# A DiT block on one core: the first head's weights split while the modulation columns load, and the upward stage in another unit order

## The chip, the cores and the metric

The kernel runs on one core of a Trainium2 chip. The metric is the device time of one execution in microseconds (us), the median of several runs; one further execution was recorded by the hardware profiler and left a trace.

## The reference

One transformer block of a diffusion model: 2048 rows of x and 256 rows of context, width 1024, 4 HGRN2 heads and 4 retention heads of width 128, a feed-forward width of 2816.

```python
mod = silu(c) @ w_mod + b_mod                    # [1024] @ [1024, 6144]; the same for c_ctx
sh1, sc1, g1, sh2, sc2, g2 = split(mod, 6)
hx = rmsnorm(x, norm1_g) * (1 + sc1) + sh1       # the same for ctx, with its own modulation
p = hx @ w_in                                    # [2048, 1024] @ [1024, 4608], for 8 heads
...                                              # bidirectional chunk scans of HGRN2 and retention,
                                                 # which start from the context's final states
x = x + g1 * (mixed @ w_out)
hx2 = rmsnorm(x, norm2_g) * (1 + sc2) + sh2
gate, up = split(hx2 @ w_up, 2)                  # [2048, 1024] @ [1024, 5632]
gate = conv3_along_rows(gate) + conv_b           # three taps for each column
x = x + g2 * ((silu(gate) * up) @ w_down)        # [2048, 2816] @ [2816, 1024]
return rmsnorm(x, final_g)
```

## The kernel before

**Products.** The large products run in f16 at close to f32 precision: each operand is scaled by a power of two and kept as a pair of f16 numbers (the rounded value and what is left of it), and one product of two blocks is three matmuls (`mm3`, L101 to L103). On top of that a 2x2 block product takes 7 block products instead of 8: rows and contraction, or columns and contraction, are halved, and sums and differences of the halves are formed. So every group of features becomes 7 feature blocks and every pair of weight tiles 7 weight blocks ("w_z", "w_q", "w_vg" for the heads, "w" for the feed-forward), each as an f16 pair. A head's weights come as raw f32 tiles of 128 columns ("raw"), are squared and summed (ssqw) for the power of two (p2s), and then *split*: rounded on ScalarE (`w <- raw, p2s`), the rest formed on VectorE by scalar_tensor_tensor (`w <- raw, p2s, w`, L697), with four subtractions of raw tiles in between.

**Program order.** The kernel is written for a tile framework: tiles live in named slots, waits are put in by dependence, and the framework's scheduler orders the instructions of each engine. Python code sets what comes early or late: generators do a piece of work per step, and `work(n)` lets those in the list `bg` do n steps between the products of a unit.

**Start.** `setup` loads small vectors; `mod_loads` queues on SyncE the first four 512-column blocks of w_mod in the order j4 = 2, 3, 0, 1 (scale, then shift), after j4 = 3 the last group of 512 rows of x (x3, the tiles "hc" and "x"), and raw weight tiles of head 0 (`items0`): z (the two forget gates), q, and v and g together (vg). `heads` calls `mod_first`, which multiplies the columns by silu(c) on TensorE and copies a row of the result from ScalarE (`modrow`, L255), then `norm_rows` (RMS norm of the rows, L398 and L407), the split of z, `lower_bounds` (a softmax, with two table loads of ScalarE), and `modulation`: the vectors A and B of the affine map, the sum of squares and maximum, a power of two s, and A and B times s. `first_blocks` makes the first seven feature blocks of rows 1536 to 2047 ("hx"): transpose the normed rows on TensorE (tp), apply the affine map (ftmp), and form the pairs: the cast on ScalarE (L434), the rest on VectorE (L435). With `early=1` the first chunk is mapped by the unscaled vectors and scaled afterwards. Then q and vg are split, and the heads' projections begin.

**Upward stage.** After the output projection the second norm makes two sets of seven feature blocks ("feat", 1024 rows each; t = 0 and 1; `second_norm_a` and `second_norm_b`, L1481 and L1504). `ffn_up` then walks 22 column tiles in 11 pairs j. For each pair there are four units: ty = 0 (gate) and ty = 1 (up), for both row sets t. A unit (j, ty, t) is 7 block products of 12 matmuls. `up_weights(j, ty)` loads two raw tiles (wur), squares them into two of its own weight tiles, sums them on TensorE (L1596) and splits them, with the four subtractions on GpSimd. Weight tiles have two sets of slots ("z" tags), so the weights of a unit pair can be made while the ones before are used. `gate_evac` applies the convolution taps (L1675 and L1676), `up_evac` multiplies, `act_pairs` forms and stores pairs of the result (st, actd).

The order of the units before is (0,0,0), (0,0,1), (0,1,0), (0,1,1), (1,0,0), ...; the features of set t = 1 are background work of the first unit.

## Time and profile before

| | |
|---|---|
| median of 3 runs | 2621.72 us (2617.08 to 2621.84) |
| profiled execution | 2617.45 us, of which the span is 2615.7 us |
| TensorE (PE) busy | 2509.6 us, 96% of the span |
| VectorE (DVE) busy | 1887.9 us, 72% |
| ScalarE (ACT) busy | 1348.6 us, 52% |
| GpSimd (POOL) busy | 424.9 us, 16% |
| DMA | queue q1 42.4% of 16 engines' time; 152 GB/s over the span |

Busy time is the union of an engine's instructions. The page also has each engine's busy share in 40 slices of the span and the clock that the throttle granted to TensorE ("PEclk"). The span begins with the first recorded instruction; the execution's own time has 1.75 us around it. The first product of the upward stage is at 1368.4 us.

### The profile page before, as it was taken

The page shows a single profiled execution, that of the slowest core. Times are in us where ns is not written, and L with a number is a line of the kernel's source. Part 1 is how long each engine was busy: PE and PEld are TensorE (multiplying, and loading weights), DVE is VectorE, ACT ScalarE, POOL GpSimd, SP SyncE. Part 2 cuts the span into 40 slices and gives each one's busy share as a digit, 9 for nine tenths or more (in the row PEclk, how much of TensorE's full clock was granted, in tenths as well). Part 3 has the DMA queues.
Part 4 walks back from the last instruction along what each step waited for, and adds up shares of the span by engine and source line. Part 5 has one row for each costly group of instructions (what it writes and reads, how often), then busy time and mean ns, then how long its engine had stood idle before and what let it go on. Part 6 is the DMA issues. An engine that isn't in the chain of part 4 may idle for free. (4 is left out here: it accounts for less than half of the span.)

```text
span 2615.7 us, 56265 instructions
## 1 busy us (share of the span) xinstructions
PE 2509.6 (96%) x22763; PEld 1653.6 (63%) x22763; DVE 1887.9 (72%) x4276; ACT 1348.6 (52%) x2877; POOL 424.9 (16%) x409
## 2 busy tenths in 40 slices
PE   5799998999999999999998999999999999999998
PEld 3689887889899999895543444444444444444443
DVE  4888786776878777785658788788888887223756
ACT  5886566564654454553646555556555554211220
POOL 1100000000000000001453433434343432000000
PEclk7999999999999999999999999999999999999999
DMA  8324442442548667794511323233333326544552
GB/s 297 122 86 164 133 143 86 135 148 73 175 163 277 210 225 242 238 343 150 170 72 57 117 89 121 89 113 105 109 105 117 111 99 232 203 175 154 210 208 86
DMA packets 218516, 402.36 MB, mean 154 GB/s; under 512 B 16143, under 2 KB 98291, under 8 KB 213648
## 3 DMA queue, kind: packets, MB, share of 16 engines
q1 hardware_dynamic: 208704, 381.81, 42.4%
q10 hardware_dynamic: 9248, 16.79, 2.0%
q8 instruction: 178, 2.92, 0.5%
q14 instruction: 82, 0.67, 0.1%
q0 software_dynamic: 304, 0.17, 0.0%
HBM read 302.77 MB, written 95.94 MB: 152 GB/s over the span
## 5 line engine op out<-in xcount | busy, mean ns | idle before, releaser
L101 PE MATMUL pa<-feat,w 128*128 128x512 f16 x704 | 265.5, 381 | 9.8 <-ACT ta L597 6.8
L102 PE MATMUL pa<-feat,w 128*128 128x512 f16 x704 | 268.2, 381 | 0.0
L103 PE MATMUL pa<-feat,w 128*128 128x512 f16 x704 | 267.6, 381 | 0.0
L102 PE MATMUL pd<-wd,actl 128*128 128x512 f16 x616 | 233.3, 379 | 0.0
L103 PE MATMUL pd<-wd,actl 128*128 128x512 f16 x616 | 233.3, 379 | 0.0
L101 PE MATMUL pd<-wd,actl 128*128 128x512 f16 x616 | 232.6, 379 | 0.0
L102 PEld LDWEIGHTS <-w 128*128 128x128 f16 x1232 | 120.7, 98 | 153.6 <-issue 15.2
L103 PEld LDWEIGHTS <-w 128*128 128x128 f16 x1232 | 120.8, 98 | 146.4 <-issue 2.1
L101 PEld LDWEIGHTS <-w 128*128 128x128 f16 x1232 | 120.7, 98 | 142.1 <-issue 2.4
L102 PEld LDWEIGHTS <-hx 128*128 128x128 f16 x1824 | 179.3, 98 | 7.3 <-issue 5.1
L101 PEld LDWEIGHTS <-hx 128*128 128x128 f16 x1824 | 179.8, 99 | 2.1
L103 PEld LDWEIGHTS <-hx 128*128 128x128 f16 x1824 | 179.4, 98 | 0.9
L1462 POOL TENSOR_TENSOR ssq<-ssq 128x1 f32<-128x1 f32 x16 | 4.2, 263 | 1066.4 <-ACT junk L1457 1066.4
L1706 DVE SCALAR_TENSOR_TENSOR st<-act,modT,st 128x512 f16<-128x512 f32 x154 | 141.2, 952 | 30.0 <-ACT st L1705 29.3
L1705 ACT ACTIVATE st<-act,modT 128x512 f16<-128x512 f32 x154 | 107.4, 717 | 105.9 <-DVE act L1695 60.4
L101 PE MATMUL pa<-w_vg,hx 128*128 128x128 f16 x800 | 143.0, 220 | 1.0 <-ACT ct L597 0.7
L102 PE MATMUL pa<-w_vg,hx 128*128 128x128 f16 x800 | 142.9, 220 | 0.0
L103 PE MATMUL pa<-w_vg,hx 128*128 128x128 f16 x800 | 142.8, 220 | 0.0
L101 PE MATMUL pc<-feat,w 128*128 128x512 f16 x352 | 133.6, 380 | 2.8 <-ACT tb L597 1.5
L102 PE MATMUL pc<-feat,w 128*128 128x512 f16 x352 | 133.6, 380 | 0.1
L103 PE MATMUL pc<-feat,w 128*128 128x512 f16 x352 | 133.7, 380 | 0.0
L101 PE MATMUL pa<-hx,w_z 128*128 128x256 f16 x464 | 127.1, 274 | 1.6 <-DVE K L639 1.2
(552 smaller groups left out, 7354.1 us busy)
## 6 DMA issues: line engine op xcount, KB each, us to landing
hx<-hxd SPq DMA_DIRECT2D x212, 512.0 KB, 5.0
actd<-st SPq DMA_DIRECT2D x154, 256.0 KB, 2.1
actl<-actd SPq DMA_DIRECT2D x28, 1024.0 KB, 5.2
wur<-in_w_up_dram SPq DMA_DIRECT2D x44, 512.0 KB, 4.1
raw<-in_w_in_dram SPq DMA_DIRECT2D x36, 512.0 KB, 4.8
wm<-in_w_mod_dram SPq DMA_DIRECT2D x64, 256.0 KB, 3.9
hxd<-hx SPq DMA_DIRECT2D x28, 512.0 KB, 4.5
wdb<-in_w_down_dram SPq DMA_DIRECT2D x44, 256.0 KB, 3.9
```

The source lines that it names most:

```text
L101: mm(ps, lhs(0), rhs(0), start=start, stop=False, skip_group_check=True)
L102: mm(ps, lhs(0), rhs(1), start=False, stop=False, skip_group_check=True)
L103: mm(ps, lhs(1), rhs(0), start=False, stop=stop, skip_group_check=True)
L1462: nc.gpsimd.tensor_tensor(ssq[:, 0:1], ssq[:, 0:1], ssq[:, 1:2], ALU.add)
L1705: nc.scalar.activation(p[:, 0], v, AF.Copy, scale=s)
L1706: nc.vector.scalar_tensor_tensor(p[:, 1], v, s, p[:, 0], ALU.mult, ALU.subtract)
```

## The change

1. The host lays out w_in, w_up (tiles of 128 columns) and w_mod (tiles of 512 columns) so that each partition's part of a tile is one piece of memory (4 KB); before, it was pieces of 512 bytes (w_in, w_up) or 2 KB (w_mod).
2. z is loaded first and split before `mod_first(2)`; x3 is loaded after the column j4 = 2; q and vg are loaded after j4 = 3, into other slots, and split before the columns 0 and 1 are worked on; `lower_bounds` and the row norm are written earlier.
3. `first_blocks(plain=True)`: all eight chunks are mapped by the unscaled vectors, the pairs of the blocks 0 and 1 are made after all transposes, and the scale s is applied in the pair itself (an activation with a scale, and scalar_tensor_tensor in the place of tensor_tensor). Six of the eight affine operations are on ScalarE, two on VectorE.
4. In the second norm the feature halves that GpSimd formed are formed by VectorE: in `second_norm_a` all, in `second_norm_b` three of the blocks.
5. The weights W(0,0) go into the slots "vg", which the heads have left; pair 1's gate weights are loaded before the last output product; the units begin (0,0,0), (1,0,0), (0,0,1), (0,1,0), (0,1,1), (1,0,1), (1,1,0), (1,1,1) and go on as before from j = 2.

Lines of the diff, without those around them (of `ffn_up` only the new body; the old one stands above):

```diff
-        wsrc = self.I["w_mod"][0].rearrange("(k p) n -> p k n", p=P)
-        self.wm = []
+        self.items0[0][0]()
+        self.wm = {}
...
+            self.wm[j4] = []
...
-                nc.sync.dma_start(w, wsrc[:, k:k + 2, 512 * j4:512 * j4 + 512])
-                self.wm += [(j4, k + i, w[:, i]) for i in range(2)]
-            if j4 == 3:
+                nc.sync.dma_start(w, self.I["w_mod"][j4, :, k:k + 2])
+                self.wm[j4] += [w[:, i] for i in range(2)]
+            if j4 == 2:
...
-            if j4 in (3, 1):
-                self.items0[0 if j4 == 3 else 4][0]()
-    def mod_first(self):
-        nc = self.nc
-        for j4, k, w in self.wm:
-            if k == 0:
-                ps = self.ps("sc", [P, 512], "mod_ps")
+            if j4 == 3:
+                self.items0[4][0]()
+                self.items0[5][0]()
+    def mod_first(self, j4):
+        nc = self.nc
+        ps = self.ps("sc", [P, 512], "mod_ps")
+        for k, w in enumerate(self.wm[j4]):
...
-            if k == KT - 1:
-                if j4 == 2:
-                    self.small_vectors()
-                self.mod_rows(ps, 2, j4)
+        if j4 == 2:
+            self.small_vectors()
+        self.mod_rows(ps, 2, j4)
...
-            cast = nc.scalar.copy(o[:, :, 0], v)
-            self.tail = nc.vector.tensor_tensor(o[:, :, 1], v, o[:, :, 0], ALU.subtract), cast
+            if plain:
+                cast = nc.scalar.activation(o[:, :, 0], v, AF.Copy, scale=s)
+                self.tail = nc.vector.scalar_tensor_tensor(o[:, :, 1], v, s, o[:, :, 0], ALU.mult, ALU.subtract), cast
+            else:
+                cast = nc.scalar.copy(o[:, :, 0], v)
+                self.tail = nc.vector.tensor_tensor(o[:, :, 1], v, o[:, :, 0], ALU.subtract), cast
...
-        b = []
+        A, B, s = self.plain if plain else self.mod1
+        late, b = [], []
...
-                    A, B, s = self.plain if k < early else self.mod1
-                    A, B = (v[:, which, kk:kk + 1] for v in (A, B))
-                    if r and g in (None, NG - 1):
-                        nc.vector.tensor_scalar(at[r], tp, A, B, ALU.mult, ALU.add)
+                    ka, kb = (v[:, which, kk:kk + 1] for v in (A, B))
+                    if r and (g is None or plain and i):
+                        nc.vector.tensor_scalar(at[r], tp, ka, kb, ALU.mult, ALU.add)
...
-                        nc.scalar.activation(at[r], tp, AF.Identity, bias=B, scale=A)
-                    if k < early:
-                        nc.vector.tensor_scalar(at[r], at[r], s, None, ALU.mult)
+                        nc.scalar.activation(at[r], tp, AF.Identity, bias=kb, scale=ka)
...
-                        pair(r, u, both[r][:, :, :n])
+                        late.append((r, u, both[r][:, :, :n]))
+                        if not plain:
+                            pair(*late.pop())
...
+        for a in sorted(late, key=lambda a: a[0]):
+            pair(*a)
...
-        src = self.I["w_in"][0].rearrange("(k p) n -> p k n", p=P)
+        src = self.I["w_in"]
...
-            own = dict(q=("ou2",), vg=("K1", "Q1")) if h == 0 else {}
+            own = dict(q=("ou2",), vg=("hx", "hx")) if h == 0 else {}
...
-                    nc.sync.dma_start(raws[-1], src[:, :, c:c + P])
+                    nc.sync.dma_start(raws[-1], src[c // P])
...
-        self.mod_first()
-        items[5][0]()
+        for _, comp in items[:4]:
+            comp()
+        self.mod_first(2)
+        self.lower_bounds()
+        self.norm_rows(NG - 1, self.x3)
+        self.mod_first(3)
+        for _, comp in items[4:]:
+            comp()
+        self.mod_first(0)
+        self.mod_first(1)
...
-        self.norm_rows(NG - 1, self.x3)
-        for _, comp in items[:4]:
-            comp()
-        self.lower_bounds()
...
-        for _ in self.first_blocks(NG - 1, self.x3, self.temps(("ou0", "ou1", "K0", "Q0")), "pj", 1):
+        for _ in self.first_blocks(NG - 1, self.x3, self.temps(("K0", "ou0", "Q0", "ou1")), "pj", True):
...
-        for _, comp in items[4:]:
-            comp()
...
-                self.feat_pair(X[r][:, k], f, self.nc.gpsimd)
+                self.feat_pair(X[r][:, k], f, self.nc.vector)
...
-            pair(X[2][:, k], b22, nc.gpsimd)
+            pair(X[2][:, k], b22, nc.vector)
...
-            pair(X[6][:, k], b12, nc.gpsimd)
+            pair(X[6][:, k], b12, nc.vector)
...
+        self.u10 = self.up_weights(1, 0)
+        next(self.u10)
...
-        self.bg = [self.second_norm_b(1, x3)]
+        self.norm_b = self.second_norm_b(1, x3)
...
-        wup = self.I["w_up"][0].rearrange("(k p) n -> p k n", p=P)
+        wup = self.I["w_up"]
...
-            nc.sync.dma_start(r, wup[:, :, ty * FF + f * P:ty * FF + (f + 1) * P])
+            nc.sync.dma_start(r, wup[ty * NF + f])
...
-        W = [self.slot_tile([P, 2, 4, P], F16, "z", "w7") for _ in range(7)]
+        W = [self.slot_tile([P, 2, 4, P], F16, "z" if j or ty else "vg", "w7") for _ in range(7)]
...
+        acts, ends = {}, {}
+        def unit(j, ty, t):
+            if ty == 0:
+                acts[j, t] = [self.slot_tile([P, 2 * G], F32, KEPT[2 * ((2 * j + t) % 3) + f], "act") for f in range(2)]
+            e = ends.setdefault(j, [{}, {}])
+            act = [acts.get((j, i)) for i in range(2)]
+            evac = self.gate_evac(j, t, act, e) if ty == 0 else self.up_evac(j, t, act)
+            for _ in self.ffn_unit(self.W[j, ty][0], self.feats[t], evac, t):
+                self.work(2)
+            if ty:
+                self.bg.append(self.act_pairs(j, t, act[t]))
+        ahead, U = self.ahead, self.up_weights
+        u10, u01 = self.u10, U(0, 1)
+        self.bg = [u10, ahead(u01), self.norm_b]
+        unit(0, 0, 0)
+        self.bg.append(u01)
+        unit(1, 0, 0)
+        u11 = U(1, 1)
+        self.bg.append(ahead(u11))
+        unit(0, 0, 1)
+        self.work(99)
+        self.bg.append(self.down_blocks(0))
+        unit(0, 1, 0)
+        unit(0, 1, 1)
+        self.work(99)
+        u20, u = U(2, 0), U(2, 1)
+        self.bg += [u11, ahead(u20)]
+        unit(1, 0, 1)
+        self.work(99)
+        self.bg += [u20, ahead(u), self.down_blocks(1)]
+        unit(1, 1, 0)
+        unit(1, 1, 1)
+        for j in range(2, NJ):
+            more = j + 1 < NJ
+            self.bg.append(u)
+            if more:
+                u = U(j + 1, 0)
+            unit(j, 0, 0)
+            self.bg += [ahead(u)] * more + [self.down_blocks(j)]
+            unit(j, 0, 1)
+            self.work(99)
+            if more:
+                self.bg.append(u)
+                u = U(j + 1, 1)
+                self.bg.append(ahead(u))
+            unit(j, 1, 0)
+            unit(j, 1, 1)
...
-    named["w_in"] = np.ascontiguousarray(named["w_in"][:, :, order])
+    tiles = lambda w, n: np.ascontiguousarray(w[0].reshape(KT, P, -1, n).transpose(2, 1, 0, 3))
+    named["w_in"] = tiles(named["w_in"][:, :, order], P)
+    named["w_up"] = tiles(named["w_up"], P)
+    named["w_mod"] = tiles(named["w_mod"], 4 * P)
```

On SyncE's queue at the very start of the program (wm: columns of w_mod; raw: head 0's weight tiles; gate: the context's rows), before:

```order
L189 DMA ident<-in_ident_dram 128x128
L273 DMA wm<-in_w_mod_dram 128x2x512 x8
L383 DMA hc_153<-in_x_dram 128x512
L383 DMA hc_154<-in_x_dram 128x512
L383 DMA hc_155<-in_x_dram 128x512
L383 DMA hc_156<-in_x_dram 128x512
L383 DMA hc_157<-in_x_dram 128x512
L383 DMA hc_158<-in_x_dram 128x512
L383 DMA hc_159<-in_x_dram 128x512
L383 DMA x_198<-in_x_dram 128x512
L735 DMA raw<-in_w_in_dram 128x8x128 x2
L273 DMA wm<-in_w_mod_dram 128x2x512 x8
L735 DMA raw<-in_w_in_dram 128x8x128
L383 DMA gate<-in_ctx_dram 128x512 x4
```

And after:

```order
L189 DMA ident<-in_ident_dram 128x128
L741 DMA raw<-in_w_in_dram 128x1024 x2
L274 DMA wm<-in_w_mod_dram 128x1024 x4
L383 DMA hc_153<-in_x_dram 128x512
L383 DMA hc_154<-in_x_dram 128x512
L383 DMA hc_155<-in_x_dram 128x512
L383 DMA hc_156<-in_x_dram 128x512
L383 DMA hc_157<-in_x_dram 128x512
L383 DMA hc_158<-in_x_dram 128x512
L383 DMA hc_159<-in_x_dram 128x512
L383 DMA x_194<-in_x_dram 128x512
L274 DMA wm<-in_w_mod_dram 128x1024 x4
L741 DMA raw<-in_w_in_dram 128x1024 x3
L274 DMA wm<-in_w_mod_dram 128x1024 x8
L383 DMA gate<-in_ctx_dram 128x512 x4
```

The two z tiles moved to the head of the queue, the rows from behind the second column to ahead of it, and the q and vg tiles to ahead of the last two columns.

On ScalarE around the copy of the last modulation column (the last L255), with the softmax of `lower_bounds` (L240, L242) and the splits of head 0's weights, before:

```order
L255 COPY modrow<-mod_ps 128x512
L455 ACTIVATE ftmp<-tp,modT,modu 128x512
L255 COPY modrow<-mod_ps 128x512
L240 ACT_TABLE_LOAD
L240 ACTIVATE tmp<-tmp 128x16
L242 ACT_TABLE_LOAD
L242 ACTIVATE table<-tmp 128x1
L743 ACTIVATE w_q,ssqw<-raw 128x1024
L696 ACTIVATE w_z<-raw,p2s 128x512 x2
L696 ACTIVATE w_z<-raw,neg 128x512
L743 ACTIVATE w_vg,ssqw<-raw 128x1024 x2
L696 ACTIVATE w_z<-raw,p2s 128x512 x4
```

And after:

```order
L702 ACTIVATE w_vg<-raw,p2s 128x512 x2
L702 ACTIVATE w_vg<-raw,neg 128x512
L255 COPY modrow<-mod_ps 128x512
L702 ACTIVATE w_vg<-raw,p2s 128x512 x4
L459 ACTIVATE ftmp<-tp,modT,modu 128x512 x2
L255 COPY modrow<-mod_ps 128x512
L240 ACT_TABLE_LOAD
L240 ACTIVATE tmp<-tmp 128x16
L459 ACTIVATE ftmp<-tp,modT,modu 128x512
L242 ACT_TABLE_LOAD
L242 ACTIVATE table<-tmp 128x1
L459 ACTIVATE ftmp<-tp,modT,modu 128x512 x3
L435 ACTIVATE hx<-ftmp,p2s 128x2x256 x8
```

The splits of z are no longer there (they stand further ahead), those of vg moved from behind the features to ahead of the last copy, and all affine operations (L459, before L455) read the unscaled vectors, with the scale p2s in the casts (L435).

On VectorE at the opening of the upward stage (L631 or L637: sums of a unit's products; L1481 and L1489: feature halves; the numbered w: weight tiles), before, where w_21587 belongs to W(0,0):

```order
L697 SCALAR_TENSOR_TENSOR w_21587<-wur,p2s,w_21587 128x512
L1465 TENSOR_SCALAR x_21932<-x_21932,rs_y 128x1024
L631 TENSOR_TENSOR ta<-pb,ta 128x512
L130 TENSOR_TENSOR both<-ssqw 128x1
L1675 SCALAR_TENSOR_TENSOR act<-ta,taps,act 128x511
L1676 SCALAR_TENSOR_TENSOR act<-ta,taps,act 128x511
L1504 TENSOR_TENSOR feat<-ftmp,feat 128x512
L1504 TENSOR_TENSOR ftmp<-ftmp 128x512
L1481 TENSOR_TENSOR feat<-feat 128x512
L1504 TENSOR_TENSOR ftmp<-ftmp,feat 128x512
L1481 TENSOR_TENSOR feat<-ftmp,feat 128x512
```

And after, where all w_2202. belong to W(1,0):

```order
L703 SCALAR_TENSOR_TENSOR w_22023<-wur,p2s,w_22023 128x512
L637 TENSOR_TENSOR ta<-pb,ta 128x512
L703 SCALAR_TENSOR_TENSOR w_22024<-wur,p2s,w_22024 128x512
L703 SCALAR_TENSOR_TENSOR w_22026<-wur,neg,w_22026 128x512
L1685 SCALAR_TENSOR_TENSOR act<-ta,taps,act 128x511
L1686 SCALAR_TENSOR_TENSOR act<-ta,taps,act 128x511
L703 SCALAR_TENSOR_TENSOR w_22027<-wur,p2s,w_22027 128x512
L703 SCALAR_TENSOR_TENSOR w_22029<-wur,p2s,w_22029 128x512
L1512 TENSOR_TENSOR feat<-ftmp,feat 128x512
L1512 TENSOR_TENSOR ftmp<-ftmp 128x512
L703 SCALAR_TENSOR_TENSOR w_22028<-wur,p2s,w_22028 128x512
L1489 TENSOR_TENSOR feat<-ftmp,feat 128x512
```

The split of pair 1's gate weights moved in between the features of row set 1 and the first unit's evacuation.

28 lines of the change are left out of this document (3 added, 25 removed).

## The prediction

> **What bounds the kernel now.** I read the share of TensorE first, over the whole span, from the page:
>
> ```profile
> span 2615.7 us, 56265 instructions
> ...
> PE   5799998999999999999998999999999999999998
> ...
> PEclk7999999999999999999999999999999999999999
> ```
>
> Then the busy time of each engine in the stretches where those digits are low (start:end, length, busy PE, PEld, DVE, ACT, POOL with counts, granted clock, DMA share, GB/s):
>
> ```profile
> 0.00:36.00 36.00, 22.55 (x103) 8.37 (x103) 4.40 (x20) 13.28 (x29) 7.26 (x21) 0.86 1.00 346
> 36.00:53.00 17.00, 8.98 (x46) 7.05 (x43) 13.44 (x53) 15.09 (x24) 0.00 (x0) 0.62 0.80 255
> 53.00:76.00 23.00, 14.54 (x80) 9.60 (x79) 23.00 (x45) 16.24 (x32) 0.00 (x0) 0.76 0.52 199
> 76.00:100.00 24.00, 22.45 (x288) 19.70 (x286) 17.86 (x36) 23.79 (x55) 5.17 (x12) 1.00 0.29 96
> ...
> 1371.00:1390.00 19.00, 19.00 (x101) 10.13 (x100) 12.95 (x18) 12.51 (x24) 6.45 (x11) 1.00 0.26 80
> 1390.00:1408.00 18.00, 10.38 (x60) 5.01 (x59) 18.00 (x30) 11.64 (x21) 5.88 (x5) 0.83 0.01 1
> 1408.00:1432.00 24.00, 22.02 (x93) 9.39 (x92) 23.11 (x44) 15.44 (x29) 12.11 (x9) 0.91 0.27 88
> 1432.00:1450.00 18.00, 16.53 (x91) 7.29 (x89) 13.76 (x27) 12.28 (x20) 6.13 (x4) 1.00 0.18 58
> 1450.00:1505.00 55.00, 49.44 (x252) 22.36 (x250) 40.09 (x68) 29.54 (x55) 23.40 (x16) 0.99 0.41 134
> 1505.00:1550.00 45.00, 45.00 (x207) 20.21 (x206) 32.77 (x57) 23.43 (x39) 13.39 (x10) 0.97 0.24 82
> ```
>
> PE is full almost everywhere; the change touches the two places where it isn't. At the start DMA is the limit until 36 us (share 1.00) while DVE works 4.4 of 36 us; from 53 to 76 DVE is the limit (23.00 of 23) and PE starves. In the upward stage (from 1371 us in these stretches) PE idles from 1390 on with DVE at 18.00 of 18. From 1371 to 1550 PE is busy 162.4 of 179 us, so 16.6 are idle, and the clock takes 10.38x0.17 + 22.02x0.09 + 49.44x0.01 + 45x0.03 = 5.6 more: about 22 us lost.
>
> **The start.** Before, the chain runs: last modulation column, its copy, the sum of squares, the power of two (p2s), features, products. From the timelines of ScalarE and VectorE (start, duration, instruction):
>
> ```profile
> 27.18 0.71 ACT L407 ACTIVATE x<-x,rs_y 128x512 f32<-128x512 f32 x1
> ...
> 36.84 0.58 ACT L255 COPY modrow<-mod_ps 128x512 f32<-128x512 f32 x1
> 37.44 1.28 ACT L240 ACT_TABLE_LOAD   x1
> ...
> 39.70 0.17 DVE L263 TENSOR_TENSOR modT<-modt_ps,sv 128x8 f32<-128x8 f32 x1
> ...
> 47.07 0.15 DVE L116 TENSOR_SCALAR p2s<-p2i 128x1 int32<-128x1 int32 x1
> ...
> 50.59 0.61 ACT L434 CAST hx<-ftmp 128x512 f16<-128x512 f32 x1
> ...
> 61.89 1.42 DVE L697 SCALAR_TENSOR_TENSOR w_vg<-raw,p2s,w_vg 128x512 f16<-128x512 f32 x2
> ...
> 66.88 1.31 DVE L435 TENSOR_TENSOR hx<-ftmp,hx 128x512 f16<-128x512 f32 x2
> ...
> 72.42 0.63 ACT L398 ACTIVATE junk<-x 128x512 f16<-128x512 f32 x1
> ...
> 73.62 0.70 DVE L435 TENSOR_TENSOR hx<-ftmp,hx 128x512 f16<-128x512 f32 x1
> ...
> 76.15 0.77 DVE L697 SCALAR_TENSOR_TENSOR w_vg<-raw,p2s,w_vg 128x512 f16<-128x512 f32 x1
> ```
>
> The copy ends at 37.4 (call it T), p2s comes 9.7 us later, the last first feature at 74.3, the last vg weight at 76.9. A pair of back-to-back operations gives the pace: scalar_tensor_tensor 0.66 us (1.42 for two, less the tail of 0.76), tensor_tensor 0.60.
>
> Moved ahead of T: the z split (7 scalar_tensor_tensors x 0.66 + 4 tensor_tensors x 0.60 = 7.0 us of DVE), the q split (1.3) and the vg split (7.0). The cover is the DVE idleness of 31.6 us up to 36, and ScalarE has 22.7 free there. Part of the cover fails: the order puts ScalarE's last four vg splits and two affine operations ahead of the last column's copy. The raw vg and q tiles are 1.57 MB (three of 0.52) and now queued ahead of the last two columns' loads. Up to them the queue carries two z tiles, two columns (2.1 MB each), the rows (2.1) and these three: 8.9 MB, at 0.346 MB/us (0 to 36) 25.8 us, and some 5 until the last lands. On ScalarE their squares follow the row norm (ended at 27.9 before) and end near 32; the scale takes 1.7; from 33.7 DVE's 1.3 + 7.0 and the hand-overs between the two engines end at 41 to 42. Then two affines of 0.7 and the copy: T = 43, 5.6 us later than before.
>
> From T to p2s the same two table loads (1.28 each) come first, and the last two of eight transposes now wait for banks that affines free, ahead of the row of the maximum: 3.6 us of tables and modT, 5 of alternating affine and transpose at half clock, 1.1 of power of two. That is 9.7 again, so p2s at 52.7. What follows is short: 14 halves now as scalar_tensor_tensor x 0.66 (scale inside: +0.06 each, 0.8 in all) and 8 subtractions x 0.60 = 14.0 us, features done at 66.8: 7.5 us earlier than 74.3. The vg work behind them is gone, 76.9 less 66.8 = 10.1 us on DVE. ScalarE, full from 76 to 100, gets its row norm (72.42) after the last cast, 52.7 + 12.5 = 65.2, and meets two vg splits of 0.7 fewer: 8.6. I take **9 us**, nearer to ScalarE's number because it is the full engine next. Bounds: if T slips only by the DMA's 2 us, 12.5; if DVE takes 4 us longer over vg, 5; the excluded side is below 0, since that needs p2s after 59.8. From there to 1200 us the order on DVE is the same row for row, so the gain is carried on; the loads of the next rows (they are queued behind the columns in either kernel, and end by about 48) aren't late.
>
> **The upward stage.** The timeline of TensorE there, with in brackets the idle time before a product and who ended it:
>
> ```profile
> 1406.13 0.59 PE L101 MATMUL pa<-feat,w 128*128 128x512 f16 x1 [5.58 <-ACT ta L597]
> ...
> 1425.63 0.38 PE L101 MATMUL pa<-feat,w 128*128 128x512 f16 x1 [1.74 <-DVE tb L631]
> ...
> 1440.57 0.38 PE L101 MATMUL pa<-feat,w 128*128 128x512 f16 x1
> 1440.78 0.38 PE L102 MATMUL pa<-feat,w 128*128 128x512 f16 x1
> ...
> 1498.74 0.23 PE L1596 MATMUL col<-onesb,w 128*128 128x1 bf16 x3 [2.70 <-ACT w L1591]
> ```
>
> Matmuls go every 0.215 us (1440.57, 1440.78). VectorE and GpSimd at the same place:
>
> ```profile
> 1371.60 0.74 DVE L697 SCALAR_TENSOR_TENSOR w<-wur,p2s,w 128x512 f16<-128x512 f32 x1
> ...
> 1378.21 0.16 DVE L130 TENSOR_TENSOR both<-ssqw 128x1 bf16<-128x1 f32 x1 [1.97 <-ACT w L1591]
> ...
> 1381.38 3.06 POOL L1481 TENSOR_TENSOR feat<-ftmp,feat 128x512 f16<-128x512 f32 x2 [6.62 <-ACT feat L1480]
> ...
> 1381.86 1.57 DVE L1481 TENSOR_TENSOR feat<-feat 128x512 f16<-128x512 f32 x1
> ...
> 1383.35 1.64 DVE L1504 TENSOR_TENSOR ftmp<-ftmp,feat 128x512 f32<-128x512 f32 x1
> ...
> 1412.30 0.69 DVE L1481 TENSOR_TENSOR feat<-ftmp,feat 128x512 f16<-128x512 f32 x1
> ```
>
> A unit (one half of a 256-column pair, one row set) is 84 matmuls, 18.1 us. Before, unit (0,0,1) is due at about 1390, when the first is through, but the last of its features lands at 1413: this is the stall (5.58 us at its longest). Now (1,0,0) stands between. In the order, PE has 184 matmuls (39.7 us), 32 transposes (4) and the weight sums (0.9) ahead of the product that needs the last feature: it is due 44.6 us after the opening. Up to that feature DVE has 43 tensor_tensors x 0.60, 21 scalar_tensor_tensors x 0.66, some 22 small operations x 0.12 (0.16 alone, a little less in a row) and four POOL subtractions of the split of pair 1 in its way: 25.8 + 13.9 + 2.6 + 4x0.9 = 46. The 0.9 is from the rows above: two POOL halves (3.06) stretch two DVE operations from 0.69 to 1.57 and 1.64, 1.83 us for two. With 3 us in which DVE has too little to do at the opening, the feature comes at 49: **4.4 us** of stall stay. The split of (0,0), which ended at 1372, is no longer in the way: its tiles are vg's, free since product 1, and it is hidden under products 2 and 3, where PE is full.
>
> The moved halves: 16 go from POOL to DVE, 8 of them in this window. Each costs 0.60 on DVE and spares it 0.9: 2.4 us less, counted in the 46. The page "SBUF — State Buffer" of the Trainium skill (the section with the single rule on the shared port pair) says that of VectorE and GpSimd the loser blocks for the other's whole instruction; by that each half would spare DVE up to 1.5 us, 3.06/2, and the sum would be 5 us lower. The rows show 0.9, and I go by them.
>
> Next late are the weights of (0,1), with DVE still full: 2 us, as the 1.74 above. Then those of (1,1): their tiles come free only after (0,1,1), so that the split has one unit (18.1 us) where others have two. Squares 2x1.25, sum and scale 2.5, seven splits paced by POOL about 9, together 14, fit alone; with the gate's evacuation and a pair's outputs on DVE I put 3 us there. The clock's part falls with the idle time, from 5.6 to about 3. Lost after: 4.4 + 2 + 3 + 3 = 12.4 against 22: a gain of **9.5 us**. Bounds: all 22 at best; at worst (1,1) late by 20 us, a loss of 8.
>
> **Contiguous loads.** The loads by their issues, with KB each and the median us to landing:
>
> ```profile
> hx<-hxd SPq DMA_DIRECT2D x212, 512.0 KB, 5.0
> wur<-in_w_up_dram SPq DMA_DIRECT2D x44, 512.0 KB, 4.1
> raw<-in_w_in_dram SPq DMA_DIRECT2D x36, 512.0 KB, 4.8
> ```
>
> Pieces of 4 KB (hx) land no sooner than pieces of 512 bytes (wur, raw) of the same size, and PE waits for wur only through the squares (2.70 above and a follower of 1.5). I take **0.5 us**, between 0 and 3. The page "DMA: Bandwidth & Descriptors" (Why small descriptors are slow) gives a fixed 3 cycles per packet: an estimate from it is 16+3 against 128+3 for 4 KB, some 14% of a transfer, 0.6 us per load and at most 2 us here. The rows don't show it.
>
> Sum: 9 + 9.5 + 0.5 = 19. The profiled execution took 2617.45 us (span 2615.7 and 1.75 around it), 4.3 below the median 2621.72, whose three runs go from 2617.08 to 2621.84. 2617.45 - 19 = **2598.5**, and I give this for the median too, with the 4.3 us left to the upper end.
>
> **Rivals.** A: only the start pays; DVE bounds the upward stage whatever the order, since it was full from 1390 to 1432 with the same work. For it: 46 against 44.6 leaves no slack. 2617.45 - 9 - 1 = 2607; chance 0.20. B: the upward stage runs almost without stalls. For it: POOL is out of DVE's way in the norm. 2617.45 - 9 - 21 = 2587; 0.13. C: the start pays little, because ScalarE and DVE were only filled earlier and T is late; against it: DVE was idle for 31.6 us there. 2617.45 - 3 - 9.5 = 2605; 0.12. D, slower: the weights of (1,1). In the kernel before the split of such weights takes long (timeline of ScalarE):
>
> ```profile
> 1454.39 1.06 ACT L1591 ACTIVATE w<-wur 128x1024 bf16<-128x1024 f32 x1 [5.74 <-DMA wur<-in_w_up_dram]
> ...
> 1493.14 0.72 ACT L696 ACTIVATE w<-wur,p2s 128x512 f16<-128x512 f32 x1
> ```
>
> 39 us from squares to last part. If that is its need and not its leisure, the unit (1,1,0) is 21 us late, its PE restarts at half clock (2 more), and 19 turns into -4: 2621.5. It decides from 19 us of lateness, and is slower by over 0.2% from 24; against it, nothing hurried that split, and its parts add to 14. 0.07 in all. E: neither part moves the end, 2615 to 2620; 0.04. The forecast, 2590 to 2604, has 0.44.
>
> **Numbers.** 0.2% (5.2 us) is about what a measurement of this kernel can tell from no change. Faster holds the forecast, A, B and C, 0.89 less a little of A for high medians: 0.90 with part of E; same 0.06; slower 0.04. The range is 2585 to 2611: B at its low end, A plus a high median at its upper; D and E stay outside.
>
> **What would show it.** Start: the last column's copy at 42 to 44 us, p2s near 53, the last first feature near 67, no vg split after 45, and DVE in 36 to 53 full. Wrong if the copy ends before 40 or p2s after 57. Upward stage: no PE stall of over 5 us in the first 45 us, the clock above 0.9, POOL without any feature halves, and (1,1,0) beginning within 4 us of the end of (1,0,1). The forecast is wrong if the transposes of the first eight blocks cost otherwise than assumed, or if ScalarE becomes the limit in the 45 us.

## The result and the profile after

| | before | after |
|---|---|---|
| median of 5 runs | 2618.05 us (2615.75 to 2621.84) | 2601.55 us (2600.16 to 2607.41) |
| profiled span | 2615.7 us | 2598.5 us |
| first product of the upward stage | 1368.42 | 1359.18 |
| from there to the end of the span | 1247.3 | 1239.3 |

The ratio is 0.9937, 95% interval [0.9921, 0.9953]: 16.5 us faster, where 19 were forecast and 2598.5 us for the time. In the traces 9.2 of the 17.2 us lie before the upward stage and 8.0 behind its first product.

The page of the kernel after, the lines that were shown of before:

```profile
span 2598.5 us, 56251 instructions
...
PE   6899998999999999999999999999999999999998
...
PEclk6999999999999999999999999999999999999999
```

TensorE's digits rise at the start (5 and 7 to 6 and 8) and from 8 to 9 in the slice at 1373 us; the clock's first digit falls from 7 to 6 (a second trace of the same kernel, below, has 8 there). By stretches (start:end, length, busy PE, PEld, DVE, ACT, POOL with counts, granted clock, DMA share, GB/s), the same at the start and the upward stage's moved 9 us forward:

```profile
0.00:36.00 36.00, 21.91 (x89) 10.78 (x89) 16.31 (x55) 24.60 (x48) 7.25 (x21) 0.78 0.97 371
36.00:53.00 17.00, 13.49 (x56) 7.30 (x56) 9.59 (x25) 11.20 (x16) 0.00 (x0) 0.60 0.70 264
53.00:76.00 23.00, 18.10 (x126) 14.04 (x126) 18.32 (x40) 18.17 (x42) 1.25 (x3) 0.75 0.40 160
76.00:100.00 24.00, 21.28 (x321) 18.76 (x319) 20.76 (x42) 23.97 (x51) 2.94 (x10) 1.00 0.44 155
...
1362.00:1381.00 19.00, 19.00 (x110) 9.75 (x107) 17.22 (x30) 12.52 (x22) 7.40 (x9) 1.00 0.14 41
1381.00:1399.00 18.00, 17.13 (x103) 9.11 (x102) 17.97 (x34) 16.11 (x32) 0.00 (x0) 1.00 0.05 22
1399.00:1423.00 24.00, 22.67 (x106) 10.18 (x104) 23.71 (x53) 16.54 (x33) 6.62 (x5) 1.00 0.20 61
1423.00:1441.00 18.00, 15.20 (x63) 6.60 (x63) 11.42 (x17) 8.39 (x14) 5.04 (x4) 0.91 0.38 110
1441.00:1496.00 55.00, 50.33 (x254) 22.46 (x252) 44.30 (x69) 27.93 (x50) 23.80 (x16) 0.97 0.36 120
1496.00:1541.00 45.00, 45.00 (x225) 20.68 (x224) 34.79 (x66) 24.01 (x41) 17.57 (x12) 1.00 0.34 113
1541.00:1600.00 59.00, 56.12 (x274) 25.34 (x273) 47.33 (x79) 36.03 (x64) 23.31 (x16) 1.00 0.31 102
```

VectorE's work moved from 53 to 76 us (23.00 of 23 before, 18.32 now) into the loads' time (16.31 instead of 4.40 up to 36 us), and the loads go at 371 instead of 346 GB/s. From 1362 to 1541, the same 179 us as before, TensorE idles 9.7 us and the clock costs 15.20x0.09 + 50.33x0.03 = 2.9: 12.6 lost, where 22 were and 12.4 were forecast. But 2.9 more are lost right behind, in the last row.

The start, from the timelines of ScalarE and VectorE:

```profile
40.96 1.41 DVE L703 SCALAR_TENSOR_TENSOR w_vg<-raw,p2s,w_vg 128x512 f16<-128x512 f32 x2
...
44.62 0.58 ACT L255 COPY modrow<-mod_ps 128x512 f32<-128x512 f32 x1 [2.10 <-PE mod_ps L290]
...
45.23 1.28 ACT L240 ACT_TABLE_LOAD   x1
...
54.08 0.15 DVE L116 TENSOR_SCALAR p2s<-p2i 128x1 int32<-128x1 int32 x1
...
65.14 4.06 DVE L436 SCALAR_TENSOR_TENSOR hx<-ftmp,p2s,hx 128x512 f16<-128x512 f32 x6
...
67.41 0.61 ACT L398 ACTIVATE junk<-x 128x512 f16<-128x512 f32 x1
```

The last copy ends at 45.2 (before 37.4, forecast 43), p2s is there at 54.1 (47.07; 52.7), the first features are done at 69.2 (74.3; 66.8), and the norm of the next rows begins at 67.4 (72.42; 65.2): each is 1.4 to 2.4 us later than forecast, and the norm has 5 us of lead where 7.2 were forecast (8.6 with the two vg splits that ScalarE is spared).

That is one execution. In the seven traces below with this start and this softmax the copy ends between 43.7 and 46.3 us and p2s comes between 52.6 and 55.1, 8.9 us behind the copy's end in each. So a shift of a microsecond of the copy alone tells nothing.

The waits of TensorE in the upward stage, all over 1 us:

```profile
1425.80 0.38 PE L101 MATMUL pa<-feat,w 128*128 128x512 f16 x1 [4.13 <-DVE tb L637]
...
1485.28 0.39 PE L103 MATMUL pc<-feat,w 128*128 128x512 f16 x1 [1.95 <-DVE w L703]
1486.95 0.39 PE L103 MATMUL pa<-feat,w 128*128 128x512 f16 x1 [1.28 <-DVE w L703]
...
1494.05 0.35 PE L1606 MATMUL col<-onesb,w 128*128 128x1 bf16 x8 [1.44 <-ACT w L1601]
...
1561.64 0.38 PE L101 MATMUL pa<-feat,w 128*128 128x512 f16 x1 [1.91 <-ACT ta L603]
```

The old wait of 5.58 us for a feature is gone, though the last feature block isn't early. Its last half, and the first of the three matmuls that need this half:

```profile
1409.27 0.68 DVE L1489 TENSOR_TENSOR feat<-ftmp,feat 128x512 f16<-128x512 f32 x1
```

```profile
1413.09 0.38 PE L101 MATMUL pc<-feat,w 128*128 128x512 f16 x1
```

The half is there at 1409.95, 50.8 us after the opening (the first product, 1359.18), and the three begin 53.9 us after it, 3.1 us later.

Of the waits listed, the first row is in unit (0,1,0), behind it the clock is at 0.91; the next three are W(1,1); the last is in (2,0,1).

### The profile page after: what moved, and what is told of

The parts are those of the page before. It is cut to its first block, busy times and chain, and to the rows that moved or that the text cites. A ratio compares the mean times of both kernels' runs of the same rounds, so it can differ in the third digit from the quotient of the medians.

```text
span 2598.5 us, 56251 instructions
## 1 busy us (share of the span) xinstructions
PE 2509.5 (97%) x22763; PEld 1655.1 (64%) x22763; DVE 1894.8 (73%) x4304; ACT 1351.5 (52%) x2880; POOL 383.0 (15%) x377
## 3 DMA queue, kind: packets, MB, share of 16 engines
q1 hardware_dynamic: 134976, 381.81, 42.4%
## 4 chain that ended last, share of the span: by engine, by line
PE 72%; DVE 11%; issue 6%; DMA 5%; ACT 4%; POOL 1%; SPq 0%; ACTq 0%; DVEq 0%; POOLq 0%
PE pa L101 8%; PE pa L102 8%; PE pa L103 8%; PE pd L103 5%; PE pd L101 5%; PE pd L102 5%; PE pc L101 4%; PE pc L103 3%; PE pc L102 3%; PE pb L101 2%; PE pb L102 2%; PE pb L103 2%; PE opp L101 2%; PE opp L103 2%; PE opp L102 2%
```

## The experiments

Each was compared with the kernel before on the same chip. For each profiled execution the table has the first product of the upward stage and the time from there to the end of the span. The first part differs by some us between executions of the same code, by single dips of the clock; the second is steadier: five traces have the changed kernel's upward stage (the result's, vg behind the columns, sigmoid alone, the changed kernel again, the filler), and they go from 1239.3 to 1241.1. Only the filler and the last two kernels of the table ran beside the changed kernel (its second run) on one chip; the others are compared with it by their ratios to before.

| kernel | median, us | ratio to before, 95% | first upward product | from there |
|---|---|---|---|---|
| loads contiguous alone | 2612.16 | 0.9978 [0.9969, 0.9987] | 1365.2 | 1244.1 |
| loads + new start | 2604.29 | 0.9948 [0.9936, 0.9961] | 1362.1 | 1242.7 |
| ... + new order, halves on GpSimd | 2599.30 | 0.9933 [0.9921, 0.9945] | 1357.6 | 1238.1 |
| ... + old order, halves on VectorE | 2599.88 | 0.9935 [0.9922, 0.9947] | 1358.8 | 1237.1 |
| changed kernel again | 2600.82 | 0.9933 [0.9921, 0.9944] | 1358.3 | 1240.9 |
| vg split behind the columns | 2601.12 | 0.9932 [0.9919, 0.9946] | 1358.6 | 1239.7 |
| softmax as a sigmoid | 2603.03 | 0.9946 [0.9930, 0.9961] | 1357.7 | 1241.1 |
| down blocks of pair 0 in pair 4 | 2600.01 | 0.9929 [0.9916, 0.9942] | 1364.7 | 1237.5 |
| W(1,1) in W(0,0)'s slots | 2609.54 | 0.9965 [0.9953, 0.9977] | 1357.3 | 1248.4 |
| filler matmuls at the start | 2601.65 | 0.9937 [0.9925, 0.9949] | 1358.9 | 1241.0 |
| sigmoid + down blocks of pair 0 last | 2591.18 | 0.9898 [0.9884, 0.9912] | 1353.3 | 1233.4 |
| that + W(1,1) in W(0,0)'s slots | 2604.64 | 0.9946 [0.9933, 0.9960] | 1359.6 | 1246.8 |

**Contiguous loads alone.** The kernel before with the host's layout and the loads that read it:

```diff
-                nc.sync.dma_start(raws[-1], src[:, :, c:c + P])
+                nc.sync.dma_start(raws[-1], src[c // P])
...
-            nc.sync.dma_start(r, wup[:, :, ty * FF + f * P:ty * FF + (f + 1) * P])
+            nc.sync.dma_start(r, wup[ty * NF + f])
```

Expected: 

> The kernel before with only the contiguous layout of w_in, w_up and w_mod. Theory (read from the two traces): the changed kernel gains 3.3 us near 1045 us, where before a weight load of a later head was late (PE waits 1.8 us for w_g's squares and the clock falls to 0.91), and the start's DMA rate is 400 to 420 GB/s where it dipped to 290 to 306; if the layout does this, this kernel is 3 to 5 us faster than before and has no such wait near 1045 us. Rival (the prediction): 0.5 us, and the 3.3 us came only from the other phase of the loads; then the wait is there still.

Measured: 5.2 us faster (3.4 to 8.1 by the interval). From 0 to 36 us the loads go at 365 GB/s where they went at 346, but the start ends no sooner, as the columns weren't what it waited for. What TensorE waits for in the upward stage, the kernel before and then this one, by engine, line, what released it, us in all, times, longest:

```profile
PE col L1596 <- ACT w L1591: 5.0, 3, 2.7
```

```profile
PE col L1595 <- ACT w L1590: 2.7, 1, 2.7
```

The squares of freshly loaded weights were late three times, now once: 2.3 of the 3.2 us gained behind the upward stage's start. The same tiles land sooner, the median of wur in 3.6 us where it was 4.1, that of raw in 4.2 where it was 4.8:

```profile
wur<-in_w_up_dram SPq DMA_DIRECT2D x44, 512.0 KB, 3.6
```

Near 1045 us I was half wrong. The wait for w_g is still there:

```profile
PE allsum L124 <- ACT w_g L742: 1.6, 1, 1.6
```

It was 1.8. What is gone is the low clock around it (0.85 and 0.81 for 10 us, 3.19x0.15 + 5.00x0.19 = 1.4 us). That is not the layout's doing alone: in the trace with pair 0's blocks in pair 4 (below), whose loads are contiguous, the wait of 1.8 us is there again at 1040, with clocks of 0.86 and 0.80. So 2.3 of the 5.2 us are traced to a wait that went, and the rest isn't.

**Loads and the new start**, with the upward stage of before (second norm, order, slots and weights' timing put back).

Expected: 

> The changed kernel with the upward stage of before (contiguous loads and the new start stay). Theory: 9 to 10 us faster than before, the first product of the upward stage at 1359, and 8 us slower than the changed kernel. Rival: the upward stage of before hides part of an earlier start, because its own loads set it; then less than 6 us faster.

Measured: 13.1 us faster than before, 7.9 more than the loads alone; 9 to 10 had been expected, and by the ratios the changed kernel is only 3 to 4 us faster still, not 8. The first upward product came at 1362.1, 3 later than expected: this execution lost 4 us between 450 and 550 us, which the two kernels below and the changed one did not. Up to there its lead over the loads alone was 6.9 us, at 150 as at 300 us. The upward stage takes 1242.7 from its first product, 1.4 less than with the loads alone.

**The new order with the halves on GpSimd** (the change but for its four lines in the second norm), and **the halves on VectorE in the old order** (the change but for `ffn_up`, the slots and the early load of W(1,0)).

Expected of the first: 

> The changed kernel with the second norm's halves back on GpSimd. Theory (the prediction's 0.9 us a half saved net of 0.6): 2 to 3 us slower than the changed kernel, with the stall at the end of the norm longer by that. Rival 1: a GpSimd half blocks VectorE for all its 1.5 us: 5 to 7 us slower. Rival 2: no difference within 1 us, because in this order the features are due late and the halves sit off the path.

Expected of the second: 

> The changed kernel with the old unit order, old slots and old weight timing, but the halves on VectorE. Theory: the features of set 1 bound the old order, so 2 to 4 us faster than the kernel with the new start alone, and 4 to 6 slower than the changed kernel. Rival: VectorE has the same work in sum and the halves move only where it waits: no faster than the new start alone.

Measured: both are as fast as the changed kernel, and each takes 4.5 to 5.6 us off the 1242.7 us by itself; both together take 1.6 to 3.4 in the five traces. The medians of the two are 5.0 and 4.4 us under 2604.29. So order and halves are two cures of one stall, and they don't add. In the old order with the halves on VectorE the wait for a feature is still there (4.71 us, where it was 5.58), and the rest of the gain is spread over the shorter waits behind it; in the new order with them on GpSimd it is gone, and the longest wait is W(1,1)'s. The one and the other:

```profile
1394.40 0.58 PE L101 MATMUL pc<-feat,w 128*128 128x512 f16 x1 [4.71 <-ACT feat L1488]
```

```profile
1486.22 0.39 PE L103 MATMUL pa<-feat,w 128*128 128x512 f16 x1 [3.88 <-DVE w L703]
```

My theory for the first fell and its second rival held: the halves cost nothing where the features are due late. That for the second was right beside the new start alone, and wrong on the changed kernel, which is no faster.

**The split of vg behind the columns.**

```diff
-        for _, comp in items[4:]:
-            comp()
         self.mod_first(0)
         self.mod_first(1)
         place = [self.gate_tile() for _ in range(4)]
         xc = self.load_rows(None, place)
+        for _, comp in items[4:]:
+            comp()
```

Expected: 

> The changed kernel with the split of q and vg written behind the last two modulation columns instead of ahead of them (their loads stay where they are). Theory: in the changed kernel the last column's data are there by about 36 us, but its matmuls stand on TensorE behind transposes whose banks wait for ScalarE's vg splits, so the copy ends at 45.2; here it ends near 40, p2s comes 3 to 5 us earlier than 54.1, and with the splits interleaved after it 1 to 4 us of that are kept. Rival 1: the loads set it, the copy stays at 44 to 45 and nothing moves. Rival 2: the split only goes behind the features again and the kernel is 1 to 3 us slower.

Measured: no difference. The copies of the last two columns, and p2s:

```profile
35.75 0.58 ACT L255 COPY modrow<-mod_ps 128x512 f32<-128x512 f32 x1 [3.92 <-PE mod_ps L290]
43.30 0.59 ACT L255 COPY modrow<-mod_ps 128x512 f32<-128x512 f32 x1 [0.38 <-PE mod_ps L290]
...
56.12 0.15 DVE L116 TENSOR_SCALAR p2s<-p2i 128x1 int32<-128x1 int32 x1
```

ScalarE is free now and waits 3.92 us for TensorE, and yet the last copy ends at 43.9, within the 43.7 to 46.3 of the traces with the splits ahead of it. p2s is 12.2 us behind the copy's end instead of 8.9, because q's and vg's splits now stand between them, and so later than in any of those traces. Of the 5 us that this costs against the result's trace up to 165 us, 1.4 are left at 300: a part of the start's lead is taken up there in any case. TensorE waits for no load there, so the loads are not the limit either; what TensorE did is the next run's question.

**Filler on TensorE.** 9 matmuls before the first column and 9 behind the row norm (128x128x512, f16), with no use of their result:

```diff
+        def warm(x, n):
+            ps = self.ps("tu", [P, 512], "warm")
+            for _ in range(n):
+                nc.tensor.matmul(ps, z0[:, 0, 0], x, start=True, stop=True, skip_group_check=True)
+        warm(z0[:, 0].rearrange("p k n -> p (k n)"), 9)
         self.mod_first(2)
         self.lower_bounds()
         self.norm_rows(NG - 1, self.x3)
+        warm(self.junk, 9)
         self.mod_first(3)
```

Expected: 

> The changed kernel with 9 + 9 matmuls of 128x128x512 in f16 whose result nobody reads, put on TensorE where it idles near 14 and 22 us. Theory: in the changed kernel the granted clock is 0.50 from 27 to 44 us though TensorE is busy, so that the last two columns' matmuls and selections take 1.9 instead of 1.05 us for four or eight; this, and not ScalarE or the loads, puts the copy's end at 45.2. With the clock at full from 26 on the copy ends at 41 to 42 and the features come 2 to 4 us earlier. Rival 1: the loads set it (they land until about 43), the copy stays at 44 to 45. Rival 2: the clock falls again at 30 to 34 in spite of the filler, since the f32 work doesn't hold it: then no gain, or 1 us lost.

Measured: nothing gained. In this execution the clock was full where it had been at half. The changed kernel in the result's trace, this one, and the changed kernel again in the trace of its second run (below), without filler:

```profile
28.00:44.00 16.00, 15.29 (x66) 8.10 (x64) 10.84 (x33) 11.37 (x19) 0.00 (x0) 0.50 1.04 398
```

```profile
28.00:36.00 8.00, 5.53 (x45) 3.28 (x41) 4.89 (x24) 7.09 (x13) 0.00 (x0) 1.00 1.03 409
```

```profile
28.00:44.00 16.00, 11.20 (x62) 5.11 (x60) 10.83 (x33) 11.30 (x19) 0.00 (x0) 0.82 1.04 400
```

So the filler isn't needed for a higher clock there, and that it raised the clock isn't shown. In the seven traces with this start and no filler the mean clock from 28 to 44 us is 0.50 three times, 0.59, 0.64, 0.82 and 0.83. The third column's 16 matmuls take 3.64 us at half clock in the result's trace and 1.92 here, but also 1.92 in the trace of the old order, which has no filler.

What the higher clock buys can be read all the same. With the filler, and in the second run of the changed kernel:

```profile
36.14 1.53 PE L260 MATMUL modt_ps<-sel,modrow 128*128 128x2 f32 x8 [2.42 <-ACT modrow L255]
...
44.06 0.59 ACT L255 COPY modrow<-mod_ps 128x512 f32<-128x512 f32 x1 [1.89 <-PE mod_ps L290]
```

```profile
41.58 0.90 PE L416 MATMUL tp<-ident,hc 128*128 128x128 f32 x3 [2.68 <-ACT ftmp L459]
```

TensorE waits 2.42 us for ScalarE's copy, which stands behind the first vg splits, or 2.68 us for the affine operations, which stand behind the last ones. The last copy ends at 44.7 with the filler and at 45.2 in the second run, at a clock of 0.82, where it ended at 45.2 at 0.50. So the theory falls: a higher clock alone doesn't move the copy clear of its spread. Rival 1 falls too, since TensorE waits for no load there. With the run before it, this speaks for two limits of nearly the same length: with ScalarE freed TensorE is busy 15.11 of the 16 us and holds the copy, with the clock freed ScalarE's splits do. Both at once weren't tried.

**The softmax as a sigmoid of the difference**, the same value for two entries.

```diff
-        nc.vector.tensor_tensor(m, a, b, ALU.max)
...
-        nc.scalar.activation(e, e, AF.Exp)
...
+        nc.vector.tensor_tensor(m, a, b, ALU.subtract)
+        nc.scalar.activation(self.lb, m, AF.Sigmoid)
```

Expected: 

> The changed kernel with the softmax over two entries in lower_bounds computed as a sigmoid of their difference: one table load (1.28 us) and six small operations fewer between the last column's copy and p2s. Theory: the affine operations that free the transposes' banks wait behind the two table loads, so p2s comes 1.3 to 2.6 us earlier relative to the copy (8.9 us before), and the kernel is faster by as much. Rival: the alternation of transposes and affines sets the 8.9 us and the tables lie beside it: under 0.5 us.

Measured: no difference in the medians that the intervals could tell.

```profile
46.07 0.59 ACT L247 COPY modrow<-mod_ps 128x512 f32<-128x512 f32 x1 [2.17 <-PE mod_ps L282]
...
53.16 0.15 DVE L116 TENSOR_SCALAR p2s<-p2i 128x1 int32<-128x1 int32 x1
```

From the copy's end to p2s are 6.5 us, since both table loads went from there; in the two further traces with the sigmoid, at the end of this section, the step takes 5.5 and 6.5. In the seven with the softmax it is 8.9, so the step is shorter by 2.4 to 3.3 us whatever the execution, at least what the theory said. The copy itself was 1.5 us later here, within its spread, so 0.9 were left, and the time shows none of it.

**The down-projection blocks of pair 0 in pair 4.** In the changed kernel, GpSimd and VectorE ahead of the wait of 4.13 us:

```profile
1417.61 1.28 POOL L1647 TENSOR_TENSOR wdb<-wdb 128x512 f32<-128x512 f32 x1
1418.84 1.72 POOL L550 TENSOR_TENSOR wur<-wur 128x512 f32<-128x512 f32 x1
1420.53 1.27 POOL L1647 TENSOR_TENSOR wdb<-wdb 128x512 f32<-128x512 f32 x1
```

```profile
1411.38 0.21 DVE L1691 SCALAR_TENSOR_TENSOR act<-edge,taps,act 128x1 f32<-128x1 f32 x1
...
1411.77 0.74 DVE L1686 SCALAR_TENSOR_TENSOR act<-ta,taps,act 128x511 f32<-128x511 f32 x1
...
1419.36 1.22 DVE L1691 SCALAR_TENSOR_TENSOR act<-edge,taps,act 128x1 f32<-128x1 f32 x1
1420.50 1.84 DVE L1686 SCALAR_TENSOR_TENSOR act<-ta,taps,act 128x511 f32<-128x511 f32 x1
1422.26 1.75 DVE L703 SCALAR_TENSOR_TENSOR w<-wur,p2s,w 128x512 f16<-128x512 f32 x1
...
1425.07 0.68 DVE L637 TENSOR_TENSOR tb<-pa,tb 128x512 f32<-128x512 f32 x1
```

Eight GpSimd subtractions stand in a row there, from 1416.4 to 1428.0, four of the split of W(0,1) (L550 is one) and four of these blocks (L1647). The same operation of VectorE takes 0.74 us ahead of them and 1.84 among them, and tb, for which TensorE waits, comes behind these.

```diff
         unit(0, 0, 1)
         self.work(99)
-        self.bg.append(self.down_blocks(0))
...
-            self.bg += [ahead(u)] * more + [self.down_blocks(j)]
+            self.bg += [ahead(u)] * more + [self.down_blocks(j)] + [self.down_blocks(0)] * (j == 4)
```

Expected: 

> The changed kernel with pair 0's down-projection blocks (four GpSimd subtractions and their loads) made in pair 4 instead of in unit (0,1,0). Theory: from 1416.8 to 1426.8 eight GpSimd subtractions in a row, four of them these, stretch VectorE's taps from 0.74 to 1.75 us, and this is the wait of 4.13 us at 1425.8 and the clock of 0.91 behind it; without them the wait is under 2 us and the kernel 2 to 4 us faster. Rival: VectorE's backlog from the features sets the wait, since it was full from 1381 on: the wait stays over 3.5 us.

Measured: the wait goes, and comes back in part where the blocks now are:

```profile
1428.12 0.39 PE L101 MATMUL pc<-feat,w 128*128 128x512 f16 x1 [0.78 <-ACT w L702]
...
1719.30 0.38 PE L101 MATMUL pa<-feat,w 128*128 128x512 f16 x1 [2.51 <-DVE tb L637]
```

So the stall is GpSimd's company, not VectorE's backlog (four squares on ScalarE moved with the blocks; the rows above show the delay on VectorE). The gain is 1.8 to 3.6 us behind the first upward product, and not to be told in the median.

**W(1,1) in the slots of W(0,0).**

```diff
-        W = [self.slot_tile([P, 2, 4, P], F16, "z" if j or ty else "vg", "w7") for _ in range(7)]
+        W = [self.slot_tile([P, 2, 4, P], F16, "vg" if j == ty and j < 2 else "z", "w7") for _ in range(7)]
...
         unit(0, 1, 0)
+        u20, u = U(2, 0), U(2, 1)
+        self.bg.append(u11)
         unit(0, 1, 1)
         self.work(99)
-        u20, u = U(2, 0), U(2, 1)
-        self.bg += [u11, ahead(u20)]
+        self.bg.append(ahead(u20))
```

Expected: 

> The changed kernel with the weights W(1,1) in the slots of W(0,0), which are free after unit (0,0,1), and their split begun one unit earlier, in (0,1,1). Theory (the prediction's third term): the waits for w at 1485.3 and 1487.0 and for its squares at 1494.1, 4.7 us in all, go, and 3 to 5 us are gained. Rival: the split then meets the features' and the pair's output work on VectorE, and the waits move to (0,1,1): within 1.5 us of the changed kernel.

Measured: 2609.54 us, 7 to 8 us slower than the changed kernel by the ratios. Theory and rival both fall: the waits at W(1,1) are gone, but from 1500 to 1570 others come to 15 us.

**The changed kernel again.** Expected: 

> The changed kernel again, beside the three others. All theories: 15 to 19 us faster than before; its waits of 4.1 us in unit (0,1,0), 3.2 + 1.4 at W(1,1) and 2.9 in (2,0,1) are there again, since they come from the order and not from chance.

Measured: 19.2 us faster than before there, with waits of 4.12 and 3.2 + 1.3 us at the same products and 2.9 us lost in (2,0,1).

**Pair 0's blocks in the last pair, with the sigmoid.** In the last pair no weights of a next one are split.

```diff
+            self.bg += [ahead(u)] * more + [self.down_blocks(j)] + [self.down_blocks(0)] * (not more)
```

Expected: 

> The changed kernel with pair 0's down-projection blocks moved to the last pair (where no weights are split) and the softmax as a sigmoid. Theory: the wait of 4.1 us and the low clock behind it go as in pair 4's case, without that case's 3.7 us at 1719, and p2s is 2.4 us closer to the copy: 6 to 8 us faster than the changed kernel. Rival: the blocks delay the start of the downward stage, whose weights need them: within 2 us of the changed kernel or slower.

Measured: 2591.18 us, 9.6 under the changed kernel on the same chip; the two intervals don't meet, and it is the fastest of all. Its start and the product that waited 4.13 us:

```profile
43.31 0.59 ACT L247 COPY modrow<-mod_ps 128x512 f32<-128x512 f32 x1 [1.07 <-PE mod_ps L282]
...
49.43 0.15 DVE L116 TENSOR_SCALAR p2s<-p2i 128x1 int32<-128x1 int32 x1
...
1416.56 0.39 PE L101 MATMUL pc<-feat,w 128*128 128x512 f16 x1 [0.77 <-ACT w L694]
```

p2s is 4.6 us earlier than 54.08, 3.3 of them from the shorter step and 1.3 from a copy at the early end of its spread, and some 4 are there up to 1000 us. Behind the first upward product it takes 1233.4, 5.9 to 7.7 less than the five traces above. The first downward product comes 823.3 us behind the first upward one, where the result's trace has 829.2, so the downward stage isn't late. The two edits weren't separated with the blocks in this place.

**The same with W(1,1) in W(0,0)'s slots**, and pair 1's blocks in the last pair too.

Expected: 

> As the one before, with the down-projection blocks of pair 1 moved to the last pair as well and W(1,1) in the slots of W(0,0), split one unit earlier. Theory: what made W(1,1)'s early split 7 us slower was that the down-projection blocks of pair 0 waited for the same slots and came at 1520 in a heap with the pairs' outputs; with the blocks gone the waits at W(1,1) go too, and 2 to 4 us more than the kernel before it are gained. Rival: VectorE can't take the split in (0,1,1) in any case: slower than the one before by 3 us or more.

Measured: 13.5 us slower than the one before (2604.64). So the theory falls, and the heap of blocks was not the reason. ScalarE waits for weights' loads at that place,

```profile
1475.04 1.06 ACT L1593 ACTIVATE w<-wur 128x1024 bf16<-128x1024 f32 x1 [2.47 <-DMA wur<-in_w_up_dram]
```

while VectorE has room (5.15 of 10 us busy from 1475 to 1485): the early split seems to hold up the loads behind it, but I have not shown that, and why it costs so much stays open.

## Why the prediction was right, and where it was not

The time was 3 us off, and the sum was right by terms that were not: forecast 9 + 9.5 + 0.5, measured by the runs 7.9 for the start, 5.2 for the loads and 3.4 for the upward stage. That two of the errors nearly cancel is luck.

1. **The start, 9 us.** The runs give 7.9 (loads alone against loads and start); in the traces the lead is 5 us at the next rows' norm and 6.2 at 300 us, and 6.9 there over the loads alone. The part from p2s on was about right: 15.1 us from p2s to the last feature (forecast 14.1). T was 2.2 us late (0.7 to 3.3 in the seven traces). I took it from ScalarE's splits alone, at TensorE's full speed; the runs speak for two limits of nearly the same length, the splits and TensorE at a clock of 0.50 to 0.83. That VectorE would be full from 36 to 53 was wrong (9.59 of 17): vg was split by 42.4, and it then waited. The 8.9 us from T to p2s (forecast 9.7) stand, and the table loads are indeed in them, which I had carried along and not asked about: without them 5.5 to 6.5.

2. **Contiguous loads, 0.5 us, between 0 and 3.** This term was the most wrong: 5.2 (3.4 to 8.1). The step that failed is a comparison of two different loads: hx in pieces of 4 KB (5.0 us) beside wur in pieces of 512 bytes (4.1), from which I read that the piece doesn't matter. The same load beside itself does differ: wur lands in 3.6 instead of 4.1 us, raw in 4.2 instead of 4.8. The loads whose squares TensorE waits for make 2.3 us of the 5.2; the higher rate up to 36 us (365 against 346 GB/s) did not end the start sooner, and where the rest comes from stays open. The page "DMA: Bandwidth & Descriptors" of the Trainium skill (Why small descriptors are slow) with its fixed cost per packet pointed the right way: the 0.6 us per load estimated from it is about what the rows show, and the 2 us in all were still too few.

3. **The upward stage, 9.5 us.** The loss in the window was forecast at 12.4 and is 12.6, but of the 9.5 some 3 belong to the loads, and 2.9 are given back in (2,0,1), which I had not looked at. Order and halves together are worth 1.6 to 3.4, and either alone 4.6 and 5.6: I had priced the old stall as if only both together would cure it. The steps: the 4.4 us of stall at the last feature did not come. VectorE's work up to it was not counted too high: the feature was there 50.8 us after the opening, and I had said 49. What was wrong is when it is due. I had its product 44.6 us after the opening, behind 184 matmuls; but there stands the rest of another, earlier block's product. The last half's block is the sixth of the unit's seven products, and the half stands behind 225 matmuls, 53.9 us after the opening in the trace. 4.13 us came instead in (0,1,0), where I had 2, from GpSimd's two jobs meeting. W(1,1) was right in its place and low in size: 3.2 + 1.4 against 3. Of the moved halves I counted one row set only: GpSimd has 377 operations where it had 409, so 32 moved; the 8 in this window were right.

4. **The rivals.** A comes closest to what the upward stage did, and its reason (VectorE full whatever the order) does not hold: with pair 0's blocks in the last pair the same order takes 1233.4 us, 9.3 less than the old stage with contiguous loads. D's place was right and its price far off, and the attempt to cure it cost 7 to 8.

VectorE beside GpSimd I had priced at 0.9 us for each GpSimd operation, and that holds: the eight subtractions stretch VectorE's operations beside them by 7.0 us in all, 1.0 to 1.1 us for one like those above (1.84 and 1.75 against 0.74), and a tap on a single column takes 1.22 us instead of 0.21. The page "SBUF — State Buffer" of the Trainium skill (SBUF: two separate sides) says that a VectorE operation with two inputs from SBUF and a GpSimd operation that reads SBUF exclude each other for the whole instruction. The rows agree, in both directions: the taps and the splits, with both inputs in SBUF, are held up, and tb, with one input from TensorE's bank pa, takes its 0.68 us among them.

## What to carry to other kernels

When two edits are meant for one stall, price them as one: the second found nothing more to gain here. Before moving work off a critical product, look up which product of the unit really needs it. Before moving background work, ask which engine it will meet: here eight GpSimd subtractions in a row cost 4 us of waiting, and moving four of them to where nothing is split gave more behind the first upward product (5.9 to 7.7 us, one trace, with the sigmoid) than order and halves together (1.6 to 3.4). Judge the layout of a load by that same load, not by another one of its size. And before an experiment on a clock that one trace shows, look at a second trace of the same kernel.

## What the hardware showed that was not expected

In the result's trace TensorE's granted clock stayed at 0.50 from 28 to 44 us though TensorE was busy 15.29 of 16 us, with f32 matmuls 32 columns wide, transposes and selections. The page "TensorE: Matmul & The Clock Gate" of the Trainium skill (What's actually happening) has full clock after one busy window of about 3.4 us; here 16 busy us did not bring it, so a busy row of the profile doesn't tell by itself that the clock will rise. Nor is it the program that decides: the same instructions in other executions had a mean clock between 0.50 and 0.83 there, and what made the difference isn't shown. At the lower clock the same 16 matmuls took 3.64 us instead of 1.92, so a price taken at full clock can be low by almost half.

VectorE's smallest operations with two inputs from SBUF were held up by as much as large ones: a tap on one column, 0.21 us alone, took 1.22 us among GpSimd subtractions of 1.3 to 1.7 us, while a copy of one column beside them (at 1417.59 us) kept its 0.14.
